# A planned two-layer encoder kernel: another beginning, another order of staging tiles, and a later start for the next third's norm

## The chip, the cores and the metric

The kernel runs on one core of one Trainium2 chip. The metric is the device time of one execution in microseconds (us). The engines are named as in the profile: PE is the matrix engine TensorE (PEld its weight loads), DVE is VectorE, ACT is ScalarE, POOL is GpSimd, SP is SyncE, which issues the DMAs.

## The reference, cut to what matters

One inference step of two layers, for a prompt of 2048 rows and a sample of 32 rows of 1024 features.

```python
# layer 0
hp = rms_norm(yp, ln_pre[0])
qa, ka, va, ga, qb, kb, vb, gb = ab_project(hp, pos, w_in_ab)       # 1024 -> 3328
oa = prompt_band(qa, ka, va, N_PREV_A, None, sinks_a)               # rotary, sliding window
ob = prompt_band(qb, kb, vb, N_PREV_B, relpos_b, None)              # chunk band, learned bias
mp = concat(oa * silu(ga), ob * silu(gb)) @ w_out_ab
yp = yp + rms_norm(mp, ln_post[0])
# layer 1
hp = rms_norm(yp, ln_pre[1])
xb, z = split(hp @ w_in_c)                                          # 1024 -> 2048
xc = causal_conv4(xb)
a, u = gates(xc)                                                    # block-diagonal, 16 blocks of 64
hs = scan(h[t] = a[t] * h[t-1] + u[t])
mp = (hs * silu(z)) @ w_out_c
yp = yp + rms_norm(mp, ln_post[1])

def rms_norm(x, g):
    return x * rsqrt(mean(x * x, -1) + EPS) * g
```

## The kernel before, in words

Everything is kept transposed: features on the 128 partitions (8 tiles of 128, index k), tokens along the free dimension. The 2084 tokens (prompt, 4 of padding, sample) are six blocks of 352 (the last 324), two blocks make a third. Every product in float32 accuracy is done as three products of a rounded part and a remainder: an operand x is split into xh (a cast) and xl = x - xh, and PE adds xh*wh, xl*wh and xh*wl. One accumulator of 352 columns takes 8 x 3 = 24 matmuls. The activations of a third stand in r0h, r0l or r1h, r1l; weights are loaded into wst and split into wh, wl.

The order of the instructions on every engine is made by a planner that runs when the program is built. Each piece of work is a generator that yields requests (`R(engines, inputs, rings)`); the planner keeps a modelled time per engine and lets the generator with the smallest priority number go whose inputs are there in the model. A request for `("V","G")` goes to DVE or POOL, whichever ends first in the model, but not to POOL while `sch.alone` is true. On the chip each engine runs its list in order and waits by semaphores. All instructions are issued from one helper, so the profile puts them all on line L106; work is told apart by the names of its tiles.

The stages:

- The beginning. `first_load` brings the first two blocks in pieces (xt, xt for block 0; xr, pt, pt for block 1). `first_split` makes r0h (ACT) and r0l (DVE), `w_first` and `w_split` split the weights. The projection starts on data that is not yet divided by its norm; `first_norm` computes the sums of squares beside it and the scale r0 (tiles r, r0b), which is multiplied in when accumulators are emptied. The first four accumulators use the attention's PSUM tiles S and T, further ones two of their own (acc).
- The projection of layer 0 (`dense_P`, 26 weight tiles of 128 columns by 6 blocks), with attention running between. Emptied accumulators pass through staging tiles: s (7), sr (3), vst, xcs (cos and sin), r0b, all in a pool on the right side of SBUF, and from there to DRAM.
- When the projection has ended, this pool is closed and another, mp, is opened in its place, with m (two of 8 x 352), sacc, r and tz. A tile laid over a former one waits for the uses of that one (`reuse_waits="tile"`). `out_part` multiplies by the output weights; `fin_out` empties its accumulators into m and sums their squares.
- Layer 1 goes by thirds: `in_part(b)` (16 weight tiles by 2 blocks, with the recurrence of 8 channel groups `fin_x`, of which the results go to r0h, r0l), then `out_part(b)`. The first two accumulators of this out_part take k = 0 to 6 first and wait for the last channel (k = 7, key `("yc", b, 7)`). `norm_proc` prepares the input of in_part(b+1): two blocks, each with four squares (ACT, into the one tile sq) and reduces (DVE, into ss), a product on PE that sums over partitions (misc), square root, reciprocal, scaling, and the split into r1h, r1l. The second block's input is loaded when the first is done. `hold` is a key that the norm awaits, after its first loads, before its first square.

Of the kernel before, what the change touches and what calls it, by code (L numbers as in the profile page):

```python
# [9 lines left out]
F32 = mybir.dt.float32  # L10
F32R = mybir.dt.float32r
AF = mybir.ActivationFunctionType
OP = mybir.AluOpType
AX = mybir.AxisListType

D = 1024
KT = 8
# [5 lines left out]
BLK = 352  # L23
# [16 lines left out]
PF, PW, PA, PAS, PT = 0, 3, 2, 1, 0.5  # L40
# [1 line left out]
PK, PV, PY = 2, 2, -1  # L42
FG = 1.0
PEMA, VPTA = 0.0, 0.03
NEARLY, C2, NWARM, PS1, PN0 = 4, 1, 8, -1.0, -1.5
PX, PXL, PXN = 0.4, 0.4, 6
PEM, VPT = 0.6, 0.06
LASTP = 3
PY2, PY3 = 0.5, 3
PWU, WAHEAD = 0.5, 0  # L50
PWK = 2.5
NQT = 3
WIN = 3.4133
GLATE = 1.0

SUBS = [[(0, 176), (176, 176)]] * 5 + [[(0, 176), (176, 148)]]

# [3 lines left out]
def f32(ap):  # L61
    return ap.bitcast(F32)
# [108 lines left out]
class Sched:  # L171
# [119 lines left out]
    def spawn(self, gen, prio):  # L291
        self.n += 1
        p = [prio, self.n, gen, None]
        p[3] = next(gen, None)
        if p[3] is not None:
            self.procs.append(p)
            self.procs.sort(key=lambda q: (q[0], q[1]))
# [106 lines left out]
def hybrid_kernel(ctx, tc, I, O):  # L404
    nc = tc.nc
    sch = Sched()
    V, A, G, PE, SP = [Eng(sch, n, e) for n, e in (("V", nc.vector), ("A", nc.scalar), ("G", nc.gpsimd),
                                                  ("PE", nc.tensor), ("SP", nc.sync))]
    ENG = {"V": V, "A": A, "G": G}
    R, spawn = Req, sch.spawn  # L410
# [10 lines left out]
    def ring(pool, shape, tag, bufs, dtype=F32):  # L421
        return Ring(sch, pool, shape, dtype, tag, bufs)
# [50 lines left out]
    wcur = [-1, 0]  # L473

    def w_use(i=None):

        if i is not None:
            wcur[0] = max(wcur[0], i)
        sch.reprio("w_split", PW if wcur[1] - 1 - wcur[0] >= WAHEAD else PWU)
        return wt.get(i)  # L480

    def w_keep(i):
# [31 lines left out]
    def w_first():  # L514

        wt[0] = h, l = whr.get(), wlr.get()
        wleft[0] = 1
        s = wst.pop(0)
        for ks in (slice(0, 4), slice(4, 8)):
            yield R("V", [("wst", 0, ks.start)])  # L520
            V.tensor_copy(h[:, ks], s[:, ks])
            yield R("V", [h])
            V.tensor_tensor(l[:, ks], s[:, ks], f32(h[:, ks]), OP.subtract)
            sch.set(("W", 0) if ks.start == 0 else ("W", 0, 4), sch.t["V"] + 0.13)
        wstr.release(s)
# [81 lines left out]
    ssr = ring(xp, [128, BLK], "ss", 2)  # L607
    rr_ = ring(xp, [128, BLK], "r", 1)
    accr = ring(pacc, [128, 512], "acc", 2)
    psr_ = ring(pmisc, [128, 512], "misc", 1)  # L610

    hlr = []
# [37 lines left out]
    def norm_ps(ps, parts, w):  # L650

        for i, x in enumerate(parts):
            PE.matmul(ps[:, :w], ones, x[:, :w], start=i == 0, stop=i == len(parts) - 1)
# [90 lines left out]
    r0, fx = [rr_.get(), None], {}  # L744
# [28 lines left out]

    def first_norm(bi):

        parts = []
        for n, (g, x, v, k0, nk) in enumerate(fx[bi]):
            sg = sr if n == 2 else ssr
            if n == 0:
                for k in range(nk):  # L780
                    yield R("G", [(("h", 0), bi, k0 + k)])
                    G.tensor_tensor(v[:, k], v[:, k], v[:, k], OP.mult)
            else:
                yield R("A", [(("h", 0), bi, k0 + nk - 1)])
                A.activation(v, v, AF.Square)
            s_, = yield R("V", [x], [sg])
            V.tensor_reduce(s_, v.rearrange("p k t -> p t k"), AX.X, OP.add)
            g.release(x)
            parts.append((sg, s_))
        ps, = yield R("PE", [x[1] for x in parts], [psr_])  # L790
        norm_ps(ps, [x[1] for x in parts], BLK)
        for g, x in parts:
            g.release(x)
        r = r0[bi]
        yield R("A", [ps], func="sqrt")
        A.activation(r, ps[:, :BLK], AF.Sqrt, bias=epsT, scale=1.0 / D)
        psr_.release(ps)
        yield R("V", [r])
        V.reciprocal(r, r)
        sch.set(("r0", bi), sch.t["V"] + 0.13)  # L800

    def y_proc(b, ri, key, free=None, then=None):

        hh, hl = RT[ri]
        todo = [(bi, t0, col, w, 4 * j) for bi, t0, col, w in cells_of(b) for j in range(2)]
        cur = {}

        def y_load():
            for n, (_, t0, _, w, k0) in enumerate(todo):
                g = xrr if b == 0 and n % 3 == 2 else xtr  # L810
                x, = yield R("SP", [("o", min(b + 1, 2)), ("z", b)], [g])
                for j, src in enumerate((oT, zT)):
                    SP.dma_start(out=x[:, 4 * j:4 * j + 4, :w],
                                 in_=src[k0 * 128:k0 * 128 + 512, t0:t0 + w].rearrange("(k p) t -> p k t", p=128))
                cur[n] = x, g
                sch.set((key, "x", n))
        spawn(y_load(), PY if b == 0 else PY2)
        for n, (bi, t0, col, w, k0) in enumerate(todo):
            yield R("V", [(key, "x", n)])
            x, g = cur[n]  # L820
            o = x[:, 0:4, :w]
            e, _ = yield R(("V", "G"), [x], cost=(0.8, 1.63))
            ENG[e].tensor_tensor(o, o, x[:, 4:8, :w], OP.mult)
            ks, cs = slice(k0, k0 + 4), slice(col, col + w)
            yield R("A", [x] + ([(free, bi)] if free else []))
            A.copy(hh[:, ks, cs], o)
            th = sch.t["A"] + 0.13
            e, _ = yield R(("V", "G"), [lambda: th], cost=(0.8, 1.63))
            ENG[e].tensor_tensor(hl[:, ks, cs], o, f32(hh[:, ks, cs]), OP.subtract)
            g.release(x)  # L830
            if n % 4 == 3:
                sch.set((key, bi), max(sch.t["V"], sch.t["G"]) + 0.13)
        if then:
            then()
# [20 lines left out]
    sp = PS.enter_context(tc.tile_pool(name="stg", bufs=1, side="right"))  # L855
# [6 lines left out]
    pS = P.enter_context(tc.tile_pool(name="pS", bufs=1, space=bass.MemoryType.PSUM))  # L862
    pT = P.enter_context(tc.tile_pool(name="pT", bufs=1, space=bass.MemoryType.PSUM))
    pO = P.enter_context(tc.tile_pool(name="pO", bufs=1, space=bass.MemoryType.PSUM))
    sr = ring(sp, [128, BLK], "s", 7)
    srr = ring(sp, [128, 2, BLK], "sr", 3, F32R)
    hlr.append(srr)
    vsr = ring(sp, [128, 3, 2, 128], "vst", 1, F32R)

    xcr = ring(sp, [128, KT, 176], "xcs", 1)  # L870
    xct = {}
    ctn = {}
    r0[1] = sp.tile([128, BLK], F32, name="r0b", tag="r0b")

    def ct_done(b, c):
        n, t = ctn.get((b, c), (0, 0.0))
# [663 lines left out]
    for b in range(3):  # L1540
        ts = list(THT[b])
# [63 lines left out]
    for _ in range(NWARM):  # L1605
        PE.matmul(warmp[:, 0:128], ones, ones, start=True, stop=True)
    psr_.release(warmp)
    spawn(w_first(), -3)
    spawn(first_split(0), -2)
    spawn(first_norm(0), PN0)  # L1610
    spawn(first_split(1), PS1)
    spawn(first_norm(1), -0.5)
    SP.dma_start(out=ident, in_=I["ident"])
    for x in qbr.idle:
# [18 lines left out]
    Q = ctx.enter_context(ExitStack())  # L1633
    mp = Q.enter_context(tc.tile_pool(name="mp", bufs=1, side="right", reuse_waits="tile"))
    ac3 = accr
    mr, sar, r2r = ring(mp, [128, KT, BLK], "m", 2), ring(mp, [128, BLK], "sacc", 2), ring(mp, [128, BLK], "r", 1)
    tzr = ring(mp, [128, BLK], "tz", 1)
    sch.cuts.update((x[2].tensor.name, (KT * BLK, BLK // 2)) for x in mr.idle)
    x2n = {}
    gr = []  # L1640
# [231 lines left out]
    def in_part(b, base, ri, yi):  # L1872
# [4 lines left out]
        def fin_x(c, bi, acc):  # L1877
# [39 lines left out]
            for h, xt in enumerate(xs):  # L1917

                tx = sch.w[xt.tensor.name] + GLATE
                p_, = yield R("PE", [lambda: tx, ("gw", b, c)], [gr[h]])  # L1920
# [99 lines left out]
    def dense_2():  # L2020
        for b in range(3):
            yield from out_part(b, base + 8 * b, b % 2, I["xT"], LN_POST, x2T, lambda k, bi, b=b: (("y", b), bi), late_m=b > 0)
            if b == 0:

                yield R("PE", [("attention",)])
        spawn(gw_proc(), 1)
        xrr.retire(eti)
        for x in extra:
            xtr.retire(x)
        b1 = base + 24  # L2030
        for b in range(3):
            sch.alone = True
            if b < 2:
                spawn(norm_proc(x2T, b + 1, LN_PRE + 1, 1, (1, b + 1), [xtr, xtr], free=("in", b), src_ready=[("x2", b + 1)],
                                hold=("part", b)), PY3)
            yield from in_part(b, b1 + 24 * b, 1, 0)
            sch.alone = False
            sch.set(("part", b))
            yield from out_part(b, b1 + 24 * b + 16, 0, x2T, LN_POST + 1, O["yT"], lambda k, bi, b=b: ("yc", b, k), late=True, final=b == 2)

    spawn(dense_2(), 9)
    sch.run(lambda: not names() & {"kq_proc", "v_proc", "proc", "reduce"})
    P.close()
# [22 lines left out]
    parts = [[x[:, 4 * i:4 * i + 4].rearrange("p k t -> p (k t)") for i in range(2)] for x in extra]  # L2066
# [126 lines left out]
```

## Time and profile before

| | |
|---|---|
| median of 3 runs | 1810.09 us (1809.11 to 1812.69) |
| the profiled execution | 1810.39 us, span 1808.6 us |
| granted PE clock, mean | 0.988 |
| PE busy | 1726.3 us, 95% |
| DVE busy | 1537.9 us, 85% |
| ACT busy | 1001.9 us, 55% |
| POOL busy | 322.1 us, 18% |
| DMA | 362.80 MB, 201 GB/s |

A row of the timeline has start, duration, engine, line, operation, tiles out<-in, shapes and count, and in brackets the idle time of the engine before it and what ended that. PE's busy time runs from a matmul's issue to its modelled end, and matmuls overlap; the distance between two starts is the better measure of their rate (0.16 us for 352 columns at full clock, 0.29 at clock 0.50).

### The profile page before, as it was taken

Reading aid. Unit: us, or ns where it says so; the run is one execution under the profiler, and the core shown is the slowest. Engines: PE = TensorE matmul, PEld = TensorE weight load, DVE = VectorE, ACT = ScalarE, POOL = GpSimd, SP = SyncE. Lnnn points to the kernel's source line nnn. Section 1 sums busy time; section 2 is a strip of 40 time slices with the busy share of each in tenths; the row PEclk is TensorE's granted clock in tenths of the full one; section 3 lists DMA queues with packets and bytes.
Section 4 is the critical chain, followed back from the end, with each engine's and each line's share of the span. In section 5 each row is a group of like instructions: output and inputs, shape, how many; then the busy total and the mean of one; then the engine's idle time right before and its main releaser. Section 6 shows DMA issues by size and latency. Waiting matters only on the chain. (4 is left out here: it accounts for less than half of the span.)

```text
span 1808.6 us, 31683 instructions
## 1 busy us (share of the span) xinstructions
PE 1726.3 (95%) x11078; PEld 1674.2 (93%) x11078; DVE 1537.9 (85%) x3228; ACT 1001.9 (55%) x2055; POOL 322.1 (18%) x285
## 2 busy tenths in 40 slices
PE   8998999999999999999997999998989999999997
PEld 7988999898899999899997999998989999999996
DVE  9889977799998769998888689999988998789945
ACT  4275543367766525766664334457754587438742
POOL 4332123322312133323124000000012000100002
PEclk9999999999999999999999999999999999999998
DMA  5787766879565268887875864674556634455466
GB/s 180 204 256 235 227 183 180 225 218 276 161 188 153 73 182 244 209 229 195 226 192 163 274 211 169 233 295 160 207 182 222 246 124 143 162 208 172 146 242 232
DMA packets 232168, 362.80 MB, mean 201 GB/s; under 512 B 36340, under 2 KB 173480, under 8 KB 231992
## 3 DMA queue, kind: packets, MB, share of 16 engines
q1 hardware_dynamic: 232008, 360.78, 64.0%
q8 instruction: 87, 1.43, 0.3%
q14 instruction: 73, 0.60, 0.1%
HBM read 255.77 MB, written 107.00 MB: 201 GB/s over the span
## 5 line engine op out<-in xcount | busy, mean ns | idle before, releaser
L106 PE MATMUL acc<-r0h,wh 128*128 128x352 f32 (+2 forms) x1832 | 592.8, 324 | 11.5 <-ACT r0h L106 10.3
L106 PE MATMUL acc<-r0l,wh 128*128 128x352 f32 (+2 forms) x1832 | 593.1, 324 | 2.1 <-DVE r0l L106 2.0
L106 PE MATMUL acc<-r0h,wl 128*128 128x352 f32 (+2 forms) x1832 | 592.6, 323 | 2.3 <-DMA wl<-wo1s 1.6
L106 PEld LDWEIGHTS acc<-r0h,wh 128*128 128x128 f32 x1832 | 347.1, 189 | 14.0 <-ACT r0h L106 11.2
L106 PEld LDWEIGHTS acc<-r0l,wh 128*128 128x128 f32 x1832 | 347.1, 189 | 4.4 <-DVE r0l L106 3.4
L106 PEld LDWEIGHTS acc<-r0h,wl 128*128 128x128 f32 x1832 | 347.0, 189 | 4.3 <-DMA wl<-wo1s 2.4
L106 PE MATMUL acc<-r1h,wh 128*128 128x352 f32 (+1 forms) x864 | 277.9, 322 | 0.6 <-ACT xb L106 0.6
L106 PE MATMUL acc<-r1h,wl 128*128 128x352 f32 (+1 forms) x864 | 277.7, 321 | 0.0
L106 PE MATMUL acc<-r1l,wh 128*128 128x352 f32 (+1 forms) x864 | 277.6, 321 | 0.0
L106 ACT ACTIVATE pt<-pt,nm 128x256 f32<-128x256 f32 (+6 forms) x272 | 170.3, 629 | 70.0 <-DVE nm L106 68.9
L106 ACT CAST pp<-T 128x256 fp32r<-128x256 f32 (+4 forms) x314 | 133.1, 439 | 74.2 <-PE T L106 62.2
L106 POOL TENSOR_SCALAR pt<-pt,rr 128x256 f32<-128x256 f32 (+5 forms) x144 | 99.3, 699 | 397.5 <-DVE rr L106 183.4
L106 PEld LDWEIGHTS acc<-r1h,wh 128*128 128x128 f32 x864 | 162.7, 188 | 0.9 <-ACT xb L106 0.9
L106 PEld LDWEIGHTS acc<-r1l,wh 128*128 128x128 f32 x864 | 162.8, 188 | 0.0
L106 PEld LDWEIGHTS acc<-r1h,wl 128*128 128x128 f32 x864 | 162.6, 188 | 0.2 <-DVE wl L106 0.2
L106 DVE TENSOR_TENSOR pp<-T,pp 128x256 fp32r<-128x256 f32 (+4 forms) x314 | 151.3, 498 | 8.6 <-ACT pp L106 6.7
L106 PE MATMUL T<-ident,pt 128*128 128x128 f32 (+1 forms) x864 | 141.7, 274 | 15.5 <-DVE pp L106 12.5
L106 PE MATMUL O<-pp,vt 128*128 128x256 f32 (+2 forms) x728 | 133.8, 307 | 8.7 <-DVE pp L106 5.8
L106 PEld LDWEIGHTS T<-ident,pt 128*128 128x128 f32 (+1 forms) x864 | 100.2, 139 | 40.6 <-DVE pp L106 20.0
L106 ACT ACTIVATE m<-acc,vec 128x352 f32<-128x352 f32 (+3 forms) x103 | 51.1, 511 | 141.3 <-PE acc L106 135.6
L106 PE MATMUL S<-kk,qa 128*128 128x320 f32 (+5 forms) x376 | 121.5, 337 | 4.5 <-issue 1.5
L106 PEld LDWEIGHTS O<-pp,vt 128*128 128x128 f32 x728 | 104.5, 189 | 13.0 <-DVE pp L106 7.1
(243 smaller groups left out, 3051.6 us busy)
## 6 DMA issues: line engine op xcount, KB each, us to landing
wst<-w_in SPq DMA_DIRECT2D x93, 512.0 KB, 4.9
wst<-wo_in SPq DMA_DIRECT2D x32, 512.0 KB, 4.1
wh<-w1s SPq DMA_DIRECT2D x32, 512.0 KB, 3.6
wl<-w1s SPq DMA_DIRECT2D x32, 512.0 KB, 4.8
wh<-wo1s SPq DMA_DIRECT2D x24, 512.0 KB, 3.8
wl<-wo1s SPq DMA_DIRECT2D x24, 512.0 KB, 4.7
kk<-kB SPq DMA_DIRECT2D x32, 320.0 KB, 4.9
vt<-vB SPq DMA_DIRECT2D x16, 640.0 KB, 4.7
```

The costliest lines, as they stand in the source:

```text
L106: r = fn(*a, **k)
```

## The change

- During the beginning, `sch.alone` is true until the second block's norm has been planned, so that requests for DVE or POOL go to DVE. The first weight split has a higher priority (`PW1`), the first norm a lower one than the second block's split (`PN0`).
- `first_norm` squares each input piece in place on ACT (before: the first piece on POOL, column tile by column tile), adds the squares with plain additions on DVE (before: one strided reduce per piece) into one tile, and gives PE one sum (before: two or three).
- The staging tiles are allocated as r0b, vst, xcs, sr, s (before: s, sr, vst, xcs, r0b), and m after sacc, r and tz (before: first).
- The norm of the next third is held until `("yc", b, 7)`, the end of the recurrence's last channel group in the plan (before: until the last matmul of in_part).

```diff
-NEARLY, C2, NWARM, PS1, PN0 = 4, 1, 8, -1.0, -1.5
+NEARLY, C2, NWARM, PS1, PN0, PW1 = 4, 1, 8, -1.0, -0.7, -1.2
-GLATE = 1.0
+GLATE, SLATE = 1.0, 1.0
...
-        sch.reprio("w_split", PW if wcur[1] - 1 - wcur[0] >= WAHEAD else PWU)
+        sch.reprio("w_split", PW1 if wcur[1] < 2 else PW if wcur[1] - 1 - wcur[0] >= WAHEAD else PWU)
...
     def first_norm(bi):
-        parts = []
-        for n, (g, x, v, k0, nk) in enumerate(fx[bi]):
-            sg = sr if n == 2 else ssr
-            if n == 0:
-                for k in range(nk):
-                    yield R("G", [(("h", 0), bi, k0 + k)])
-                    G.tensor_tensor(v[:, k], v[:, k], v[:, k], OP.mult)
-            else:
-                yield R("A", [(("h", 0), bi, k0 + nk - 1)])
-                A.activation(v, v, AF.Square)
-            s_, = yield R("V", [x], [sg])
-            V.tensor_reduce(s_, v.rearrange("p k t -> p t k"), AX.X, OP.add)
+        todo = []
+        for g, x, v, k0, nk in fx[bi]:
+            yield R("A", [(("h", 0), bi, k0 + nk - 1)])
+            A.activation(v, v, AF.Square)
+            todo.append((x, v))
+        x0, v0 = todo[0]
+        for (x, v), ks in [(todo[0], slice(2, 4))] + [(z, slice(k, k + 2)) for z in todo[1:] for k in range(0, z[1].shape[1], 2)]:
+            yield R("V", [x0, x])
+            V.tensor_tensor(v0[:, 0:2], v0[:, 0:2], v[:, ks], OP.add)
+        s_, = yield R("V", [x0], [ssr])
+        V.tensor_tensor(s_, v0[:, 0], v0[:, 1], OP.add)
+        for g, x, _, _, _ in fx[bi]:
             g.release(x)
-            parts.append((sg, s_))
-        ps, = yield R("PE", [x[1] for x in parts], [psr_])
-        norm_ps(ps, [x[1] for x in parts], BLK)
-        for g, x in parts:
-            g.release(x)
+        ts = sch.w[s_.tensor.name] + SLATE
+        ps, = yield R("PE", [lambda: ts], [psr_])
+        norm_ps(ps, [s_], BLK)
+        ssr.release(s_)
...
         sch.set(("r0", bi), sch.t["V"] + 0.13)
+        if bi:
+            sch.alone = False
...
-    sr = ring(sp, [128, BLK], "s", 7)
+
+    r0[1] = sp.tile([128, BLK], F32, name="r0b", tag="r0b")
+    vsr = ring(sp, [128, 3, 2, 128], "vst", 1, F32R)
+
+    xcr = ring(sp, [128, KT, 176], "xcs", 1)
     srr = ring(sp, [128, 2, BLK], "sr", 3, F32R)
     hlr.append(srr)
-    vsr = ring(sp, [128, 3, 2, 128], "vst", 1, F32R)
-
-    xcr = ring(sp, [128, KT, 176], "xcs", 1)
+    sr = ring(sp, [128, BLK], "s", 7)
...
-    r0[1] = sp.tile([128, BLK], F32, name="r0b", tag="r0b")
...
     psr_.release(warmp)
+    sch.alone = True
...
-    mr, sar, r2r = ring(mp, [128, KT, BLK], "m", 2), ring(mp, [128, BLK], "sacc", 2), ring(mp, [128, BLK], "r", 1)
+    sar, r2r = ring(mp, [128, BLK], "sacc", 2), ring(mp, [128, BLK], "r", 1)
     tzr = ring(mp, [128, BLK], "tz", 1)
+    mr = ring(mp, [128, KT, BLK], "m", 2)
...
                 spawn(norm_proc(x2T, b + 1, LN_PRE + 1, 1, (1, b + 1), [xtr, xtr], free=("in", b), src_ready=[("x2", b + 1)],
-                                hold=("part", b)), PY3)
+                                hold=("yc", b, KT - 1)), PY3)
             yield from in_part(b, b1 + 24 * b, 1, 0)
             sch.alone = False
-            sch.set(("part", b))
```

## The prediction

> **What bounds the kernel now.** I read the table of stretches first, to see which stages TensorE (PE) does not fill. Its columns are the stretch and its length, busy time of PE, of its weight loads, DVE, ACT and POOL, then PE's granted clock, the DMA share and GB/s.
>
> ```profile
> span 1808.6 us, 31683 instructions
> ...
> 60.00:984.00 924.00, 889.10 (x5943) 849.68 (x5942) 801.49 (x2129) 522.95 (x1311) 256.79 (x241) 1.00 0.71 201
> 984.00:1000.00 16.00, 11.12 (x52) 10.46 (x51) 8.33 (x13) 4.62 (x8) 4.60 (x1) 0.79 0.87 259
> 1330.00:1345.00 15.00, 10.36 (x48) 9.99 (x49) 9.59 (x11) 6.98 (x12) 2.76 (x2) 0.77 0.47 163
> ```
>
> PE is the bound: in the long stretch of 924 us it idles 34.9 us in small pieces. The change touches four places: the beginning, the two short stretches above, each of which idles PE some 5 us and then runs it at a reduced clock, and a smaller one like them at 1540. All of it is PE time, so what is freed there moves the end, unless a later wait takes it back. The sum is made against the profiled execution's own 1810.39 us (span 1808.6), which is 0.3 us above the median of the three runs shown, 1810.09; these spread over 0.2%, so 0.2%, 3.6 us, is about what can be told from no change.
>
> **First part: the beginning.** The waits of PE from 7 to 36 us, and what DVE, POOL and PE's norm sums do between 5 and 36 us (groups of one shape: count, busy us, mean ns):
>
> ```profile
> PE S L106 <- DVE r0l L106: 3.3, 3, 1.9
> PE S L106 <- ACT r0h L106: 1.5, 1, 1.5
> PE misc L106 <- DVE ss L106: 1.5, 1, 1.5
> PE T L106 <- DVE r0l L106: 0.6, 1, 0.6
> ```
> ```profile
> L106 DVE SCALAR_TENSOR_TENSOR r0l<-xt,vec,r0h 128x352 fp32r<-128x352 f32 x8 | 8.3, 1097 | 0.0
> L106 DVE TENSOR_REDUCE ss<-xt 128x352 f32<-128x1408 f32 x2 | 5.2, 2642 | 0.0
> L106 DVE SCALAR_TENSOR_TENSOR r0l<-xr,vec,r0h 128x352 fp32r<-128x352 f32 x4 | 3.1, 833 | 0.0
> L106 DVE SCALAR_TENSOR_TENSOR r0l<-pt,vec,r0h 128x352 fp32r<-128x352 f32 x4 | 3.1, 808 | 0.0
> L106 DVE TENSOR_REDUCE ss<-xr 128x352 f32<-128x1408 f32 x1 | 2.8, 2821 | 0.0
> ...
> L106 DVE TENSOR_REDUCE ss<-pt 128x352 f32<-128x704 f32 x1 | 1.0, 956 | 0.0
> L106 DVE TENSOR_REDUCE s<-pt 128x352 f32<-128x704 f32 x1 | 0.9, 945 | 0.0
> ```
> ```profile
> L106 POOL TENSOR_TENSOR wl<-wst,wh 128x1024 fp32r<-128x1024 f32 x3 | 7.7, 2574 | 2.6 <-ACT wh L106 2.6
> ```
> ```profile
> L106 PE MATMUL misc<-ss,onesr 128*128 128x352 f32 x8 | 3.2, 502 | 1.6 <-DVE ss L106 1.5
> ```
> ```profile
> L106 DVE TENSOR_TENSOR wl<-wst,wh 128x1024 fp32r<-128x1024 f32 x2 | 2.4, 1218 | 0.0
> L106 DVE SCALAR_TENSOR_TENSOR s<-acc,r 128x352 f32<-128x352 f32 x2 | 1.1, 526 | 0.5 <-PE acc L106 0.4
> ```
> ```profile
> 987.05 0.88 DVE L106 TENSOR_TENSOR xt<-xt 128x704 f32<-128x704 f32 x1
> ```
>
> The last two fences are prices from later stretches (46 to 60 us, in which POOL has little to do, and 987 us): a DVE weight remainder 1.22, a two-input DVE operation of 352 columns 0.52, of 704 columns 0.88. DVE works without a gap through this beginning, and the 16 remainders r0l take 8.3 + 3.1 + 3.1 = 14.5 us where 16 x 0.5 = 8 would do: they stretch while POOL runs its two-input operations. DVE's ledger under the change: stretch gone, -6.5; reduces gone, -(5.2 + 2.8 + 1.0 + 0.9) = -9.9; two norms of three 704-wide adds and one 352-wide, 2 x (3 x 0.88 + 0.52) = +6.3; three weight remainders moved from POOL, 3 x 1.22 = +3.7. Net -6.4.
>
> PE's ledger: of the waits, 3.3 + 1.5 + 0.6 = 5.4 less the first remainder's 1.0, which stays (its data lands no sooner), and the 1.5 on the first r0h, also unchanged, is not counted: 4.4. Each norm's partial sums now enter PE as one product of two instructions: the eight over ss become four, -1.6 (the two over s, not counted, go too). One stretch of reduced clock, the first row here, goes with the wait before it:
>
> ```profile
> 15.80:19.20 3.40, 3.29 (x10) 2.84 (x11) 3.40 (x3) 2.92 (x5) 0.00 (x0) 0.50 0.75 282
> 1541.60:1545.00 3.40, 3.38 (x11) 3.38 (x12) 2.79 (x4) 2.37 (x5) 0.00 (x0) 0.50 0.30 22
> 1545.00:1548.40 3.40, 3.40 (x23) 3.40 (x23) 1.25 (x1) 1.26 (x2) 0.00 (x0) 1.00 0.71 289
> ```
>
> In 3.4 us at clock 0.50 PE issues 11 matmuls, at 1.00 23: such a stretch costs between 1.5 (11 matmuls, each about 0.14 late) and 1.8 us; I take 1.5. PE could gain 4.4 + 1.6 + 1.5 = 7.5. But soon after, PE needs DVE to empty its accumulators, and DVE is only 6.4 earlier, less some waiting for ACT's squares (two more of them, 1.4 us each by the one over xt, on an ACT with room). I take **-6**, between 0 (next paragraph) and -7.5.
>
> The stretch put down to POOL could have another reason; then the ledger is -9.9 + 6.3 + 3.7 = +0.1 and the gain is nothing: that is a rival. The Trainium skill, "Perfetto Trace Analysis", section Optimizing Scalar/DVE Operations, says that with a saturated DVE, handing work to ScalarE or even GpSimd may make sense, and then that between DVE and GpSimd it might not help because they share a port. By its first half the change goes the wrong way here and the sum would lack these 6 us; the trace's stretched remainders side with the second.
>
> The other edits here: the earlier split of weight 1 (PW1) only reorders; the second input half's remainders going before the norm (PN0) delay the scale r0, which PE needs only when the early accumulators must be emptied, four later: hidden by DVE's 6.4. SLATE holds one PE product 1 us; PE has the next accumulator to work on. The input tiles released later are next loaded for the norm planned at 110 us: no cost. POOL being barred until the second norm ends costs DVE the +3.7 counted above.
>
> **Second part: the order of the staging tiles.** At the change from projection to output, m is laid over tiles that the projection's staging used:
>
> ```profile
> 985.44 0.46 SPq L106 DMA_DIRECT2D zT<-s  x1
> ```
> ```profile
> 990.99 0.56 ACT L106 ACTIVATE m<-acc,vec 128x352 f32<-128x352 f32 x1 [5.54 <-DMA xt<-zT]
> ```
> ```profile
> 992.62 0.66 PE L106 MATMUL acc<-r0h,wh 128*128 128x352 f32 x1 [4.61 <-ACT r0h L106]
> ```
>
> ACT waits 5.54 us for a landing (the row names the transfer issued just before; the one that reads a tile under m is zT<-s). Queued behind it on ACT is the r0h cast whose input was ready at 987.93 (the 0.88 row above), and PE waits for that cast 4.61 us. With s allocated last and m after the small tiles, the first m lies over older staging tiles (xcs and sr) and only the second one, an accumulator (24 matmuls, about 4 us) later, over s. Then m can be written when PE's accumulator ends, about 988.2, its two ACT operations take 1 us, the cast 0.8: r0h at 990.0, PE waits 2.0. Saved 2.6, and the two reduced-clock stretches behind the old wait (clock 0.79 over 16 us) 2 x 1.5 = 3.0 if 2.0 us is too short to bring them. **-5.5**; ends -2.5 (they stay) and -7.6 (no wait either).
>
> **Third part: the norm behind the last channel.** In thirds 0 and 1 PE waits for the last recurrence channel while DVE runs the next third's reduces between that channel's steps:
>
> ```profile
> 1330.83 1.33 DVE L106 TENSOR_REDUCE ss<-sq 128x176 f32<-128x704 f32 x1
> 1332.09 0.88 DVE L106 SCALAR_TENSOR_TENSOR ti<-ti,ex 128x704 f32<-128x704 f32 x1
> 1333.08 1.36 DVE L106 TENSOR_REDUCE ss<-sq 128x176 f32<-128x704 f32 x1
> ```
> ```profile
> 1333.83 0.66 PE L106 MATMUL acc<-r0h,wh 128*128 128x352 f32 x1 [3.90 <-ACT r0h L106]
> 1335.30 0.66 PE L106 MATMUL acc<-r0l,wh 128*128 128x352 f32 x1 [0.81 <-DVE r0l L106]
> ```
> ```profile
> 1540.22 0.43 PE L106 MATMUL acc<-r0h,wh 128*128 128x352 f32 x1 [1.83 <-ACT r0h L106]
> 1541.62 0.66 PE L106 MATMUL acc<-r0l,wh 128*128 128x352 f32 x1 [0.98 <-DVE r0l L106]
> ```
>
> Third 1: without the reduces the chain is about 2.8 us shorter, PE's wait of 1.83 + 0.98 goes to about 0.3, and the reduced-clock row above (1.5) goes: **-4** (ends -1 and -4.3). The Trainium skill, "TensorE: Matmul & The Clock Gate", Part 1, puts the throttle behind an idle window of about 3.4 us; by that these 2.8 us of idle would bring no throttle and the term would be -2.5. The trace shows clock 0.50 right behind them, so I keep the row.
>
> Third 0: two reduces of 1.35 (one earlier one overlaps a wait for the table load) and a square on ACT leave the chain: PE waits about 1.9 instead of 4.7, saving 2.8, and two reduced-clock stretches, 3.0: -5.8. But the norm now begins late, and its other end is tight:
>
> ```profile
> 1324.38 0.78 ACT L106 ACTIVATE sq<-xt 128x704 f32<-128x704 f32 x1
> ```
> ```profile
> 1394.38 0.32 PE L106 MATMUL acc<-r1h,wh 128*128 128x352 f32 x1
> ```
> ```profile
> 1396.16 0.89 DVE L106 TENSOR_TENSOR r1l<-xt,r1h 128x704 fp32r<-128x704 f32 x1
> ```
>
> The first square starts at 1324.4, the last remainder of the norm's second block ends at 1397.05, and PE, which starts the next third at 1394.4, wants that block one accumulator later, about 1398.5. After the change the first square can start at about 1332, 7.8 us later; run without the channel between, its four squares and reduces take some 2.5 us less; other waits inside the norm may give 2 or 3 back. So its end is 2.5 to 5 us later and PE is 5.8 us earlier: PE waits about 5 and pays another stretch or so of reduced clock. Given back 5 + 2 of 5.8: **+1**. Ends: -5.8 (norm in time) and +8 (all 7.8 us of delay stay: wait 10.9, clock 3.0). In third 1 there is room for the same delay, as no weights are split there any more:
>
> ```profile
> 1589.21 1.46 DVE L106 TENSOR_TENSOR r1l<-xt,r1h 128x592 fp32r<-128x592 f32 x2 [0.45 <-ACT r1h L106]
> ```
> ```profile
> 1599.10 0.32 PE L106 MATMUL acc<-r1h,wh 128*128 128x352 f32 x1
> ```
>
> Its second block ends at 1590.7, and PE wants it one accumulator after 1599.1, 12 us later: 5 of delay and 4 of PE's gain fit.
>
> Sum: 1810.4 - 6 - 5.5 - 4 + 1 = **1796**.
>
> **Rivals.** (a) The norm of third 0 is in time, because it no longer shares DVE with the channel: 1796 - 6.8 = 1789. For it, the block has waits to give; against, 1.4 us of slack. (b) It keeps all its delay: 1796 + 7 = 1803. (c) The remainders' stretch is not POOL's doing, the beginning gains nothing: 1802. (d) The plan of all that follows is made anew from other start times, and the 34.9 us of idle in the 924 us of attention grow. The trace cannot show how far; it could as well shrink. From +11 us the gain is inside 0.2%, from +18 the kernel is slower, say 1816 at +20: half as much idle again. Each wait in there is short, which speaks against it.
>
> **How the numbers follow.** Forecast 0.40 (its own range 1791 to 1800), (a) 0.17, (b) 0.13, (c) 0.12, (d) ending within 0.2% 0.10, slower 0.08. Faster is the first four: 0.82. The range 1786 to 1808 leaves out (d)'s slower part, a little of its rest and the best ends of (a).
>
> **What would show it.** Right: in the first 36 us POOL idle, r0l near 0.5 us each, no clock 0.50 after 15 us; the first m written about 1 us after its accumulator; no reduce over sq between the last channel's steps, PE's waits on r0h there under 2 us. The given-back term shows as a wait of acc on r1h or r1l at the next third's start, some 62 us on. Wrong: that wait beyond 10 us, or idle in the attention stretch above 45 us.

## The result, and the profile after

The changed kernel takes 1797.58 us (median of 5 runs, 1795.19 to 1799.42) against 1810.77 us for the kernel before on the same chip: ratio 0.992, interval 0.9907 to 0.9934, 13.2 us faster. On another chip it came out at 0.9942 (0.9929 to 0.9955; 1798.71 against 1808.2 us). The profiled execution took 1799.42 us (span 1797.6), so the pair of traces differs by 11.0 us. The forecast was 1796. The sum came out, its terms did not: the beginning was given 6 us and brings next to nothing in the traces, and third 0, which was to lose 1 us, gains 2 to 4. All ratios compare fast runs: one of the twelve runs of `hold_third0` (below) took 6394 us and is left out of its ratio.

The stretches of the kernel after, in the columns of the table of before (stretch, length, busy time of PE, weight loads, DVE, ACT and POOL, then PE's clock, DMA share, GB/s):

```profile
60.00:984.00 924.00, 890.54 (x5915) 847.21 (x5913) 801.75 (x2136) 522.14 (x1313) 243.26 (x231) 0.99 0.71 200
984.00:1000.00 16.00, 13.43 (x72) 12.80 (x73) 9.77 (x13) 5.67 (x11) 4.61 (x1) 0.89 0.87 262
1326.00:1341.00 15.00, 11.46 (x60) 10.93 (x60) 13.15 (x14) 5.40 (x11) 0.14 (x1) 0.89 0.54 188
```

PE idles 33.5 us in the long stretch instead of 34.9, so the remade plan cost nothing there. In the stretch at 984 PE issues 72 matmuls instead of 52 and its clock is 0.89 instead of 0.79. At the last channel of third 0 (4 us earlier than before) the clock is 0.89 instead of 0.77: one stretch of clock 0.50 where there were two.

**The beginning.** Groups of one shape between 5 and 36 us (count, busy us, mean ns), then three stretches, PE's largest wait, SP's last stores of q before its first loads, and the first product of attention with qb:

```profile
L106 DVE SCALAR_TENSOR_TENSOR r0l<-xt,vec,r0h 128x352 fp32r<-128x352 f32 x8 | 4.2, 581 | 0.3 <-ACT r0h L106 0.3
L106 DVE SCALAR_TENSOR_TENSOR r0l<-xr,vec,r0h 128x352 fp32r<-128x352 f32 x4 | 2.1, 581 | 0.5 <-ACT r0h L106 0.5
L106 DVE SCALAR_TENSOR_TENSOR r0l<-pt,vec,r0h 128x352 fp32r<-128x352 f32 x4 | 2.1, 577 | 0.0
```
```profile
15.80:19.20 3.40, 3.40 (x23) 3.40 (x22) 3.40 (x7) 3.40 (x7) 0.00 (x0) 1.00 0.74 291
37.00:40.50 3.50, 1.33 (x10) 1.08 (x8) 3.50 (x5) 1.86 (x5) 1.48 (x2) 1.00 0.30 107
40.50:43.90 3.40, 3.40 (x13) 3.40 (x13) 3.34 (x8) 1.98 (x3) 0.00 (x0) 0.50 0.47 143
```
```profile
39.42 0.43 PE L106 MATMUL acc<-r0h,wh 128*128 128x352 f32 x1 [2.17 <-DVE s L106]
...
69.11 1.23 SPq L106 DMA_DIRECT2D qA<-sr  x2
...
77.65 0.33 PE L106 MATMUL S<-kk,qb 128*128 128x128 f32 x1 [0.72 <-DMA qb<-qA]
```

The remainders r0l take 8.4 us in all instead of 14.5, and clock 0.50 after 15 us is gone. Then DVE works 3.50 of 3.50 us while PE waits 2.17 us for DVE to empty an accumulator, and the stretch of clock 0.50 that was removed at 15.8 stands at 40.5 instead. The rest of PE's lead goes after that. The load of qb is issued at 72.96 here and at 72.97 before, and the same product waits for it until 77.65 here and, in the next fence, 77.61 before.

```profile
68.37 1.23 SPq L106 DMA_DIRECT2D qA<-sr  x2
...
77.61 0.33 PE L106 MATMUL S<-kk,qb 128*128 128x128 f32 x1 [0.70 <-DMA qb<-qA]
```

The rows of SP say why the load is no earlier. In both kernels the loads of k and q stand in SP's list behind the stores of q, and the first one follows the last store at once (70.38 here, 69.64 before). The plan made anew puts ten stores ahead of them here, before it was eight. The last two wait until DVE has finished sr at 69.08; the two before them are out at 66.44. All seven traces with this beginning have ten stores there, the five with the old one eight. No run tests this order by itself.

**The transition.** ACT's and PE's rows after, and the stretch behind them:

```profile
988.69 0.55 ACT L106 ACTIVATE m<-acc,vec 128x352 f32<-128x352 f32 x1 [2.60 <-PE acc L106]
989.49 0.78 ACT L106 CAST r0h<-xt 128x704 fp32r<-128x704 f32 x1
```
```profile
990.32 0.42 PE L106 MATMUL acc<-r0h,wh 128*128 128x352 f32 x1 [1.66 <-ACT r0h L106]
991.60 0.43 PE L106 MATMUL acc<-r0l,wh 128*128 128x352 f32 x1 [0.86 <-DVE r0l L106]
```
```profile
992.80:996.20 3.40, 3.40 (x14) 3.29 (x13) 0.90 (x1) 0.36 (x1) 0.00 (x0) 0.50 0.97 329
```

m now waits for PE's accumulator, no longer for a landing; PE waits 2.5 us instead of 4.6, and one stretch of clock 0.50 is left.

**Third 0 and third 1.** The last channel of third 0, the norm's last remainder and the start of the next third, then the one wait left near the last channel of third 1:

```profile
1323.75 2.39 POOL L106 TENSOR_TENSOR wl<-wst,wh 128x1024 fp32r<-128x1024 f32 x1 [332.95 <-DVE wh L106]
1323.96 3.66 DVE L106 TENSOR_TENSOR_SCAN ti<-ex,hcar,ti 128x704 f32<-128x704 f32 x1
...
1329.35 0.42 PE L106 MATMUL acc<-r0h,wh 128*128 128x352 f32 x1 [3.03 <-DVE r0h L106]
1330.27 0.43 PE L106 MATMUL acc<-r0l,wh 128*128 128x352 f32 x1 [0.50 <-DVE r0l L106]
...
1387.43 0.32 PE L106 MATMUL acc<-r1h,wh 128*128 128x352 f32 x1
...
1389.24 0.88 DVE L106 TENSOR_TENSOR r1l<-xt,r1h 128x704 fp32r<-128x704 f32 x1
...
1541.65 0.99 PE L106 MATMUL misc<-xs,onesr 128*128 128x352 f32 x2 [1.20 <-DVE xs L106]
```

The next third starts at 1387.43 with no wait at all. Its norm ends at 1390.12, about 1.5 us before PE wants the second block (an accumulator, some 4 us, after its start). In third 1 the two waits at 1540 are gone.

### The profile page after: what moved, and what is told of

It reads as the page before. It is cut to its first block, busy times and chain, and to the rows that moved or that the text cites. A ratio compares the mean times of both kernels' runs of the same rounds, so it can differ in the third digit from the quotient of the medians.

```text
span 1797.6 us, 31658 instructions
## 1 busy us (share of the span) xinstructions
PE 1725.4 (96%) x11072; PEld 1671.1 (93%) x11072; DVE 1537.3 (86%) x3238; ACT 1000.1 (56%) x2060; POOL 299.1 (17%) x267
## 5 line engine op out<-in xcount | busy, mean ns | idle before, releaser
L106 POOL TENSOR_TENSOR wl<-wst,wh 128x1024 fp32r<-128x1024 f32 x34 | 84.4, 2481 | 462.2 <-DVE wh L106 349.3
```

What stands on the lines that cost most here:

```text
L106: r = fn(*a, **k)
```

## The experiments

All are compared with the kernel before, run in turns on the same chip. Beside the time, a position is used: the moment at which PE has started a given amount of matmul work (each matmul by its columns, warm-up left out). One position of one trace wanders by 2 to 3 us in attention, so the position is averaged over the kernels that have a part and those that have not.

### One part at a time

`begin_only`, the first part alone (the diff's `first_norm`, PW1, PN0, SLATE and the two lines on `sch.alone` of the beginning):

> The kernel before with the first part alone (no GpSimd until the second input norm, plain sums, first weights split earlier). Theory of this study: the beginning really runs about 7 us ahead of before at 37 us, but attention's first passes cannot take it and the lead is gone by 110 us; time 1809 to 1812, no gain. Rival, the prediction's own term: the lead stays and the time is 1804 to 1805. Told apart by the time and by TensorE's start of one and the same accumulator at 37 us and at 350 us: 7 us early and then level by the theory, early at both by the rival.

Measured: ratio 0.9984 (0.9971 to 0.9997), 1805.55 us.

`order_only`, the order of the staging tiles alone:

> The kernel before with the new order of the staging tiles alone. Theory: m is written within about 3 us of its accumulator, TensorE waits 1.7 + 0.9 instead of 4.6 and one of two half-clock stretches goes; 3.4 us gained, 1807. Rival, the prediction's term: both stretches go, 5.5 us, 1805.

Measured: ratio 0.9985 (0.9972 to 0.9999), 1805.03 us.

`hold_only`, the hold alone:

> The kernel before with the norm of the next third held behind the last recurrence channel, alone. Theory: third 0 gains 3.9 us, nothing is given back at the next third's start because the norm takes 60 us instead of 72, third 1 gains 4.3; 1802.5. Rival, the prediction's terms +1 and -4: 1807 to 1808, with a wait of about 5 us on r1h or r1l at the next third's start.

Measured: ratio 0.9956 (0.9941 to 0.9972), 1801.49 us.

`order_hold`, the changed kernel with the beginning of before:

> The changed kernel with its first part undone (order and hold alone). Theory: all of the gain is here, 1797 to 1799.5, the same as the changed kernel. Rival, the beginning's 6 us are real: 1803 or more.

Measured: ratio 0.9939 (0.9919 to 0.9959), 1798.1 us; the changed kernel has 0.992 and 0.9942 on two chips. So nearly all of the gain is in the order and the hold.

`hold_third0`, the hold in third 0 only:

```
-  hold=("part", b)), PY3)
+  hold=("yc", b, KT - 1) if b == 0 else ("part", b)), PY3)
```

> The kernel before with the hold of the next third's norm in third 0 alone; third 1 as before, everything else as before. Theory: third 0 gains 3 to 4 us at the last channel (TensorE's waits there near 2.7 + 0.5 instead of 3.9 + 0.8 and one half-clock stretch less), nothing is given back at the next third's start, and TensorE's waits of 1.83 + 0.98 at 1540 us stay: ratio to before 0.9978 to 0.9985. Rival, the prediction's term: the gain is given back by a wait of about 5 us on r1h or r1l at the next third's start, and the ratio is 1.000 to 1.001.

Measured: ratio 0.998 (0.9968 to 0.9991), 1805.43 us, and its trace:

```profile
1329.88 0.43 PE L106 MATMUL acc<-r0h,wh 128*128 128x352 f32 x1 [2.29 <-DVE r0h L106]
1330.81 0.66 PE L106 MATMUL acc<-r0l,wh 128*128 128x352 f32 x1 [0.50 <-DVE r0l L106]
...
1387.66 0.32 PE L106 MATMUL acc<-r1h,wh 128*128 128x352 f32 x1
...
1533.69 0.43 PE L106 MATMUL acc<-r0h,wh 128*128 128x352 f32 x1 [2.02 <-ACT r0h L106]
```

The wait at the last channel of third 0 is smaller, the next third starts without one, and third 1 keeps its wait (2.02 us, 1.83 before). This is the theory's picture, not the prediction's term. What `hold_only` has beyond this, 0.998 to 0.9956 or some 4.3 us, is third 1.

The positions give the same split, as differences of means with their standard errors:

| part | with | without | difference |
|---|---|---|---|
| beginning, at 32 us | 7 traces | 5 | -7.6 (0.4) |
| beginning, at 66 us | 7 | 5 | -3.8 (0.3) |
| beginning, at 100 us | 7 | 5 | -0.8 (0.4) |
| beginning, at 463 us | 7 | 5 | +0.2 (1.0) |
| order, 964 to 1036 us | 7 | 4 | -3.6 (0.3) |
| third 0, 1137 to 1457 us | 8 | 3 | -2.4 (1.0) |
| third 1, 1498 to 1662 us | 8 | 4 | -3.4 (0.3) |

### Where the beginning's lead goes

`start_pe_late`: `NWARM` 8 becomes 26, nothing else.

> The changed kernel with 18 more of the warm-up products at the start, so that TensorE begins its first sums 3 us later (by the trace 20 of its matmuls at 0.16). Theory: TensorE's lead of 7 us at 37 us is not used, DVE is what must be ahead there; the wait of 2.2 us at 39 us and the half-clock stretch behind it take the delay up, and the time is within 1.5 us of the changed kernel, 1796 to 1799. Rival: the lead is real to the end and the 3 us are paid, 1800.5.

Measured: ratio 0.9963 (0.995 to 0.9977), 1803.26 us, slower than theory and rival said. The edit did not do what it was meant to: PE runs at full rate when the first sums begin (matmuls of 352 columns start 0.16 us apart from 9 us on; in the changed kernel 0.30 until 13 us), and at 32 us it stands 1.4 us ahead of the mean of the changed beginnings. Even so it is 2.8 us behind them at 50 us:

```profile
37.47 0.55 PE L106 MATMUL misc<-ident,s 128*128 128x128 f32 x3 [2.25 <-DVE s L106]
41.55 0.66 PE L106 MATMUL acc<-r0h,wh 128*128 128x352 f32 x1 [3.54 <-DVE s L106]
...
80.86 0.33 PE L106 MATMUL S<-kk,qb 128*128 128x128 f32 x1 [0.73 <-DMA qb<-qA]
```

An earlier PE only waits longer for DVE here (5.8 us), and the load of q comes 3.2 us later, behind ten stores as in the changed kernel. PE is still 2.8 us behind the mean of the changed beginnings at 463 us in this trace.

`start_dve_late`: the add that ends the first norm's sums is done eleven times instead of once.

```
-  V.tensor_tensor(s_, v0[:, 0], v0[:, 1], OP.add)
+  for _ in range(1 if bi else 11):
+      V.tensor_tensor(s_, v0[:, 0], v0[:, 1], OP.add)
```

> The changed kernel with the one 352-wide add that ends the first norm's plain sums repeated ten times more on DVE (the same value written again), 10 x 0.52 = 5.2 us more of DVE work at 21 us and nothing else. Theory: DVE sets the time from 30 to 45 us, so TensorE stands 4 to 5 us later at 50 us; and the start of attention takes most of it up, as it took up the lead of 2.7 us at 50 us between before and after: 0 to 2 us slower at the end. Rival, a time lost or won in the beginning stays to the end: 4 to 5 us slower than the changed kernel.

Measured: ratio 0.9982 (0.9971 to 0.9994), 1804.52 us; the changed kernel beside it, `changed_again`, 0.9942:

> The changed kernel once more, beside the other runs of this chip, with nothing edited: 1796 to 1799, ratio to before 0.991 to 0.9935.

```profile
48.44 0.66 PE L106 MATMUL acc<-r0h,wh 128*128 128x352 f32 x1 [6.78 <-DVE s L106]
```

5.2 us more on DVE put PE 9.3 us back at 50 us (its wait for DVE is 6.8 us instead of 2.2): DVE does set the time up to the first products, but the run is no clean test of it: only 5.2 of the 9.3 us are the added work, and the plan made anew has eight stores ahead of the loads of q, as before the change. Of these 9.3 us, 2.0 are left at 463 us in the trace, so most is taken up there; but the time is 5.8 us longer than `changed_again`, near what the rival said. The two don't agree, and this stays open: the plan of all that follows is made anew, and a median over 12 runs sees more than one trace. The same holds for `begin_only`, whose time is 2.9 us shorter while its kind of beginning shows no lead at 463 us. By the times of `begin_only` and of `order_hold` beside the changed kernel, the beginning's worth lies between 0 and 3 us; that its 7.6 us don't last is shown.

### The last channel and the norm's margin

`last_split_later`: one weight's split held, in the plan, behind the last channel of third 0.

```
+  if i == 3 * N0 + 42:
+      yield R("V", [("yc", 0, KT - 1)])
   e, (h, l) = yield R(("A", "V"), [("wst", i), ...
```

> The changed kernel with one weight's split (its cast on DVE and its remainder on GpSimd) held behind third 0's last recurrence channel, so that neither stands ahead of the scan nor runs beside it. Theory: the scan takes 1.7 us again instead of 3.66, the cast's 0.69 goes from the chain, TensorE's waits of 3.03 and 0.50 there fall under 1 in all, and the half-clock stretch behind them goes; 3 to 4.5 us faster than the changed kernel, 1793 to 1795. Rival: the norm held behind the channel has no slack, the gain comes back as a wait on r1h or r1l at the next third's start and the time stays at 1796 to 1798. Second rival: GpSimd does not stretch the scan, which stays at 3.7; at most 0.7 us.

Measured: ratio 0.9932 (0.9913 to 0.9952), 1796.88 us, no different from the changed kernel. The edit missed its aim:

```profile
1318.88 2.67 POOL L106 TENSOR_TENSOR wl<-wst,wh 128x1024 fp32r<-128x1024 f32 x1 [330.50 <-ACT wh L106]
1319.33 3.70 DVE L106 TENSOR_TENSOR_SCAN ti<-ex,hcar,ti 128x704 f32<-128x704 f32 x1
```

The hold moves an instruction's place in its queue; ACT's and POOL's queues were empty there, so the cast and the remainder ran as soon as their data was in. (The first square of the changed kernel's norm does the same: held behind the channel in the plan, it runs at 1320.28.)

`scan_alone`: the same hold, and cast and remainder of this one weight on DVE.

```
-  e, (h, l) = yield R(("A", "V"), [("wst", i), ...
+  e, (h, l) = yield R(("A", "V") if i != 3 * N0 + 42 else ("V", "V"), [("wst", i), ...
...
-  e, _ = yield R(("V", "G"), [h], ...
+  e, _ = yield R(("V", "G") if i != 3 * N0 + 42 else ("V", "V"), [h], ...
```

> The changed kernel with the same weight's split held behind third 0's last channel and put on DVE whole, so that it cannot start earlier than DVE's own order lets it and GpSimd stands still beside the scan. Theory: the scan takes 1.7 us instead of 3.7, TensorE's waits of 3.03 + 0.50 there fall by 2 or a little more, to 1 to 1.5, the half-clock stretch behind them may go (1.5); 2 to 3.5 us faster than the changed kernel. Rival: the scan is 3.7 us for another reason (its shape or place) and stays so. Second rival: the gain is there at 1335 us and is given back by the next third's start, where the norm ends only 1.5 us before it is wanted.

Measured: ratio 0.9944 (0.9929 to 0.996), 1799.62 us, `changed_again` beside it 0.9942:

```profile
1323.54 1.68 DVE L106 TENSOR_TENSOR_SCAN ti<-ex,hcar,ti 128x704 f32<-128x704 f32 x1
...
1327.39 0.43 PE L106 MATMUL acc<-r0h,wh 128*128 128x352 f32 x1 [0.97 <-DVE r0h L106]
1328.31 0.43 PE L106 MATMUL acc<-r0l,wh 128*128 128x352 f32 x1 [0.50 <-DVE r0l L106]
...
1340.13 0.43 PE L106 MATMUL misc<-xs,onesr 128*128 128x352 f32 x1 [2.47 <-DVE xs L106]
```
```profile
1340.10:1343.50 3.40, 3.24 (x11) 3.00 (x11) 3.30 (x4) 0.56 (x1) 0.00 (x0) 0.55 0.45 178
```

The scan is back at 1.68 us, and PE's first wait falls by 2.06. All of it is given back 13 us later: DVE now has the split between the norm's reduces, PE has the norm's sum next in its queue and waits 2.47 us for it, and a stretch of low clock follows that wait. This is the second rival's mechanism, at another place than it named.

`norm_later`: the norm held 6 us (of the plan) longer.

```
   yield R("A", [hold])
+  ts = sch.key[hold] + 6.0
+  yield R("A", [lambda: ts])
```

> The changed kernel with the next third's norm held some 4 to 6 us longer behind the last channel (its squares and reduces go behind the first two outputs' work). Theory: in third 0 the norm ends 1.5 us before TensorE wants its second block, so most of the delay appears as a wait of 2.5 to 4.5 us on r1h or r1l at the next third's start, with a stretch of reduced clock; in third 1 there is room; 1800 to 1804. Rival: the norm has more waits to give (as the first delay of some 8 us was taken up), no such wait, 1797 to 1799.

Measured: ratio 1.0052 (1.0033 to 1.0071), 1818.45 us, some 20 us slower than the changed kernel:

```profile
1385.13 1.25 DVE L106 RECIPROCAL ss<-ss 128x176 f32<-128x176 f32 x1
...
1397.91 1.24 DVE L106 SCALAR_TENSOR_TENSOR xt<-xt,vec,ss 128x176 f32<-128x176 f32 x4
```
```profile
1405.06 0.66 PE L106 MATMUL acc<-r1h,wh 128*128 128x352 f32 x1 [16.72 <-ACT r1h L106]
```

The theory had the place and missed the size. The first reduce starts 9.6 us after PE has taken up the last channel (1325.05 to 1334.63), 8.8 us later than in the changed kernel (1329.35 to 1330.13), so the edit delays more than it was meant to; with a margin of 1.5 us that would be a wait of some 7 us. Up to the last reciprocal the delay stays 9 us. But the norm now falls behind the end of the output's accumulators, whose scaling stands ahead on DVE: the eight scalings that in the changed kernel follow this reciprocal at once, at 1381.46, start 11.5 us behind it here. In this run a step lies beyond the margin, not a slope.

### The transition

`transition_split_later`: one weight's split held behind the last of the output's input, so that POOL stands still.

```
+  if i == 3 * N0 + 2:
+      yield R("V", [(("y", 0), 1)])
```

> The changed kernel with one weight's split (cast on DVE, remainder on GpSimd) held behind the output input's second block at the change from projection to output. Theory: DVE's product before the r0h cast starts 0.7 us earlier, r0l takes 0.88 instead of 1.25 as GpSimd is idle, TensorE's waits of 1.66 + 0.86 fall to about 1.5 in all and the half-clock stretch behind them goes; 2 to 3 us faster than the changed kernel, 1794.5 to 1796. Rival: ACT still writes m ahead of the cast, the waits stay above 2 and the stretch stays; no more than 0.5 us.

Measured: ratio 0.9924 (0.9905 to 0.9943), 1795.22 us, no different from the changed kernel.

```profile
986.60 0.88 DVE L106 TENSOR_TENSOR xt<-xt 128x704 f32<-128x704 f32 x1
988.00 0.55 ACT L106 ACTIVATE m<-acc,vec 128x352 f32<-128x352 f32 x1 [2.58 <-PE acc L106]
988.79 0.78 ACT L106 CAST r0h<-xt 128x704 fp32r<-128x704 f32 x1
989.61 0.89 DVE L106 TENSOR_TENSOR r0l<-xt,r0h 128x704 fp32r<-128x704 f32 x1 [2.13 <-ACT r0h L106]
```
```profile
989.62 0.43 PE L106 MATMUL acc<-r0h,wh 128*128 128x352 f32 x1 [1.67 <-ACT r0h L106]
```

r0l takes 0.89 us instead of 1.25 and PE's second wait falls from 0.86 to 0.50, but the first wait is unchanged: the cast's input is there at 987.48 and the cast waits until 988.79 behind m, which waits for PE's accumulator. That is the rival's reason.

## Why the prediction was right, and where it was not

**The beginning, -6.** On DVE the first step held: remainders at 0.58 us each with POOL idle until 30 us, no clock 0.50 at 15.8, and PE 7.6 us ahead at 32 us, where the ledgers gave 6.4 to 7.5. The step that failed is the last one, "DVE is only 6.4 earlier": when DVE empties the first accumulator of acc it is only 4.0 us earlier (38.86 against 42.87). PE's 2.17 us at 39.42 and the clock behind it leave 3.8 (mean), and the load of q, written and read back, comes at the same 73 us, with two more stores ahead of it; at 100 us 0.8 is left. The ledger followed the two engines to the first wait and no transfer behind it. The term is 0 to -3, the end that the prediction gave to its rival (c), but not for (c)'s reason: POOL did stretch DVE.

The Trainium skill, "SBUF — State Buffer", section "SBUF: two separate sides", says that a DVE operation with two SBUF inputs and a GpSimd operation that reads SBUF lock each other out: the one that starts first holds the port for the whole instruction. The scans agree: 1.68 us alone (`scan_alone`), 3.66 in the changed kernel beside POOL's 2.39, which starts first there, and the stretched scan ends at 1327.62, close to the end of POOL's operation plus 1.68 (1326.14 + 1.68 = 1327.82). In `begin_only` the scan starts first, at 1326.70: it takes 1.67, and POOL's operation, started at 1326.92, takes 3.62.

**The order, -5.5.** Right in mechanism, too large by 2: -3.6 by position, -2.7 by time. m waits for its accumulator and is written by 989.24, 0.6 us behind it, r0h at 990.27 where 990.0 was worked out. Two parts are mis-sized. The step did not have the second wait of 0.86 for r0l, so the waits fall by 2.1 us and not 2.6; some 0.36 of it is POOL's 4.61 us remainder beside r0l, as `transition_split_later` without it still has 0.50. The reduced clock was given 3.0 for two stretches, and the positions leave some 1.5 for it (the last section says why).

**Third 0, +1.** The step that failed is the one that gave back 5 + 2 us: the norm was not late. It now takes 60.0 us from first reduce to last remainder (1330.13 to 1390.12), against 71.7 before (1325.31 to 1397.05). It shares DVE with no channel, two small adds went from POOL to DVE, and its second block starts sooner. Before, the last reduce of the first block up to the square root:

```profile
1335.30 1.38 DVE L106 TENSOR_REDUCE ss<-sq 128x176 f32<-128x704 f32 x1
1336.76 0.94 POOL L106 TENSOR_TENSOR ss<-ss,ss 128x352 f32<-128x352 f32 x1 [346.63 <-DVE ss L106]
1338.53 1.83 POOL L106 TENSOR_TENSOR xs<-ss,xs 128x352 fp32r<-128x352 f32 x1 [0.83 <-ACT xs L106]
1344.68 0.56 ACT L106 ACTIVATE ss<-misc,epsT 128x352 f32<-128x352 f32 x1
```

After:

```profile
1338.39 1.45 DVE L106 TENSOR_REDUCE ss<-sq 128x176 f32<-128x704 f32 x1 [0.15 <-ACT sq L106]
1339.88 0.53 DVE L106 TENSOR_TENSOR ss<-ss,ss 128x352 f32<-128x352 f32 x1
1341.03 0.52 DVE L106 TENSOR_TENSOR xs<-ss,xs 128x352 fp32r<-128x352 f32 x1
1343.05 0.55 ACT L106 ACTIVATE ss<-misc,epsT 128x352 f32<-128x352 f32 x1
```

From the last reduce to the square root it takes 3.2 us instead of 8.0, and the four reduces ahead of it take 1.7 us less. Of the rest, 4.4 us lie between the blocks: the second block's first square comes 0.8 us after the first block's last remainder (1362.88), before it was 5.2 (1370.87); its first load is issued at 1357.87, before at 1364.92. Why SP comes to this load sooner no run isolates. The step counted 2.5 us for squares and reduces and "2 or 3" for waits, 5.5 at most; 11.7 came. So the mechanism of rival (a) is what happened at this place: the term is -2.4 by position, -3.6 by the time of `hold_third0`. (Of the three traces without the hold, `begin_only` has one stretch of clock 0.50 there instead of two and is 3 us shorter; against the other two the term is -3.4.) It is less than (a)'s -5.8 because POOL's remainder, which before fell elsewhere, stretched the scan by 2.0 us and PE still waits 3.5, where the prediction wanted under 2. The price named for a late norm was if anything low, as `norm_later` shows.

**Third 1, -4.** Right: -3.4 by position, about -4.3 by times. Both waits and the low clock went; a wait of 1.20 for the norm's sum came in at 1541.65.

**The sum.** Measured by position: 0.2 - 3.6 - 2.4 - 3.4 = -9.2, against -14.5 in the prediction's sum and 9.5 to 13.2 by time on two chips. The sum of 1796 held because the errors of the first two terms (6 and 2 us too much) and of the third (3.4 us too little) partly cancel, and the times show 0.3 to 4 us more than the positions. That it came within 2 us is in part luck: with the 9.5 us of the second chip the same sum would have met 1801.

## What to carry to other kernels

In these runs an engine that was ahead kept its lead only until the next place where another engine, or a transfer in its queue, was the bound. Follow a lead forward to the first row where both kernels start the same instruction at the same time, before it is put into a sum. A hold in a plan moves a place in a queue and stops nothing on an engine whose queue is empty; to keep an operation off a stretch, put it on the engine that is busy there, or make it wait for data. Work moved behind a critical chain has a margin at its other end: read that margin in microseconds, and look at what stands behind it in the queue, since missing it can cost far more than the delay.

## What the runs showed of the hardware

Whether a stretch of clock 0.50 stands behind a short wait is not set by the wait's length alone. With waits of 1.66 to 1.67 and 0.85 to 0.89 us at the transition, the changed kernel shows one (above) and `order_only` does not, here its stretch behind the waits:

```profile
989.20:992.60 3.40, 3.00 (x19) 2.71 (x18) 0.89 (x1) 0.47 (x1) 0.00 (x0) 1.00 0.97 325
```

Of six traces with this pair of waits, two have such a stretch and four have not. What tells them apart is where the waits lie on a fixed grid of time. In each of the 14 traces all stretches of reduced clock up to 1780 us start whole multiples of 3.413 us apart (in the changed kernel at 40.5, 78.0, 320.4, 429.6, 992.8, 1228.3 and 1330.7 us). Cut by this grid into windows, from 15 to 1780 us, the traces show one rule for windows at full clock. Where PE is busy less than 0.44 of the window, the next one runs at clock 0.50 (81 of 81). Where it is busy more than 0.505, the next one does not (0 of 7014). Between the two it does in 7 of 22. Here is the window that holds most of the two waits, first in the changed kernel, then in `order_only`:

```profile
989.39:992.80 3.41, 1.62 (x8) 1.39 (x9) 2.05 (x2) 1.29 (x3) 1.41 (x1) 1.00 0.50 128
```
```profile
986.17:989.58 3.41, 1.93 (x10) 1.69 (x11) 2.11 (x2) 1.23 (x2) 1.10 (x1) 1.00 0.51 114
```

PE is busy 1.62 of 3.41 us in the first, a share of 0.48, and 0.42 in `changed_again`; in the four traces without a stretch it is 0.57 to 0.61. In all six a border between two windows falls into the first wait. In the two with a stretch 0.9 to 1.1 us of this wait lie behind the border, in one window with the second wait; in the four without, 0.5 to 0.6 us. Even PE's wait of 2.89 us that ends at 984.04 in the changed kernel brings no stretch: a border at 982.56 halves it, and both windows are busy more than 0.56.

So a short wait costs 1.5 us of clock where about half of one window is idle, and nothing where a border splits the idle time. A shift of a few us moves the waits on the grid, so a sum made before the change can't tell which it will be: the second term should have carried these 1.5 us as a chance and not a price.

The Trainium skill, "TensorE: Matmul & The Clock Gate", Part 1, calls the activity window free-running and what is seen at a kernel's start run-variable; these traces agree, with windows of 3.413 us. By its idle window of about 3.4 us there would be no stretch of clock 0.50 behind any of these waits; the rows at 40.5 (one wait of 2.17) and 992.8 show one, so here half an idle window was enough.
